# Sums for the norms: fp32 products of the squares in place of reduced products of their two parts

## The chip, the cores and the metric

The kernel runs on one core of one Trainium2 chip. The metric is the device time of one execution in microseconds.

## What is computed

Two transformer blocks run one after the other on 512 tokens of 1024 features, all in fp32. The change concerns the norms of both blocks. There are norms over all features, over the 128 features of a head and over its 64 features:

```python
def rms_norm_2(x, g):
    xf = x.astype(jnp.float32)
    y = xf * lax.rsqrt(jnp.mean(xf * xf, axis=-1, keepdims=True) + EPS)
    return (y * g.astype(jnp.float32)).astype(x.dtype)

# block 1: differential attention, two softmax maps a head, their difference normed
yb = rms_norm(yb, diff_subln_g[l], SUBLN_EPS) * (1.0 - lam_init)
x = x + rms_norm(merged @ w_out[l], norm_mix_post_g[l])
h = rms_norm(x, norm_ffn_pre_g[l])
f = (jax.nn.silu(h @ w_gate[l]) * (h @ w_up[l])) @ w_down[l]
x = x + rms_norm(f, norm_ffn_post_g[l])
# block 2: gated linear attention beside dilated attention
o = rms_norm_2(o, norm_g).reshape(B, S, H * GLA_DV)
qa = rms_norm_2(aq.reshape(B, S, ATTN_HEADS, ATTN_HEAD_DIM), q_norm_g[l])
ka = rms_norm_2(ak.reshape(B, S, ATTN_HEADS, ATTN_HEAD_DIM), k_norm_g[l])
```

## The kernel before, in words

Activations lie feature-major: a tile has 128 features on the partitions and 512 tokens in its columns. Dense products take 128x128 weight tiles, streamed in chunks of eight (L237), and are exact to fp32 by parts: each operand is a high part in the reduced format fp32r and a low part, the remainder (ScalarE copies, VectorE subtracts; L251 and L125 for the weights), and a product is three reduced products (`mm3`): high by high, high by low, low by high.

A norm needs sums over the features, so over the partitions. `square` makes the squares on ScalarE; where several feature tiles are summed, GpSimd or VectorE adds their squares first (`gather`, L320). `parts` splits the squares: a copy on ScalarE to `sqh` (L308), a subtraction on VectorE to `sql` (L125). `colsum` then takes 128 tokens at a time as weights and two columns of ones as the moving operand, once with the high and once with the low part; the sums are in the PSUM bank `pc`, a token to a partition. `headsum` does the same with `hsel`, whose two columns each select half of the partitions: for norms over 64 features, and for the diagonal of the linear attention. A group of sums for 512 tokens is eight products. From the bank follow `rstd` (VectorE L334, GpSimd L336), transposes that spread the factors again (`bcast`; for 64-feature norms the copy at L1267 and transposes), and the scaling.

The program is emitted by a planner. Tasks (one head's attention, a norm, a linear attention's levels) are generators; each `yield t` says that its next TensorE work is ready t us later, on a clock `pt` that the planner advances by an assumed cost of each TensorE instruction (`pin`). Ready tasks go first, tiles of dense products fill the rest, and the order found so is fixed on TensorE. The other engines take their instructions in the order in which they are emitted. Each engine runs in order and waits by semaphores.

The stages, in us of the profile: the start and block 1's attention up to about 340, its branch products, the bridge to the feed-forward around 400 to 440, the feed-forward to 720, the bridge to block 2 to 830, block 2's mixer (linear attention, dilated attention) to 1100, a third bridge to 1150, and the last feed-forward. A bridge (`bridge`) computes the last tiles of a product in two halves of 256 tokens, so that one half's norm lies beside the other's products; its norm is `chain`. In the bridge to block 2 three sums are taken at once (`a0`, `a1`, `a2`). In the mixer, `near` makes decayed queries and keys for one level of the linear attention, `gla` multiplies them into masked scores (twelve products of 128 columns a level), `qk_norm` norms the queries and keys of the dilated attention. `decay` holds the only full fp32 products, 16 rows of weights by 512 columns, for the gates.

Of the kernel before, what the change touches and what calls it, by code (L numbers as in the profile page):

```python
# [19 lines left out]
TB = S // 128  # L20
# [22 lines left out]
# cost of a transpose on the tensor engine, for the order in which its work is issued  # L43
# [3 lines left out]
class Done:  # L47
    """Marks a piece of work as issued; `at` is when its result should be there."""
# [10 lines left out]
class Item:  # L59
    """A dense tile product: runs whenever no task has tensor work that is ready."""  # L60
# [5 lines left out]
class Emitter:  # L66
# [25 lines left out]
    def phase(self, order=range(NSLOT)):  # L92
        """A part of the program with its own use of the working tiles."""
        self.slot, self.turn, self.free = {}, {}, list(order)
        self.pfree, self.pslot, self.res["prob"] = [0, 1, 2], {}, 3

    def W(self, tag, dt=F32, b=1, shape=(128, 512)):
        """A working tile; `b` of a tag take turns."""
        n = self.turn[tag] = self.turn.get(tag, -1) + 1
        key = (tag, n % b)  # L100
        if key not in self.slot:
            self.slot[key] = self.free.pop(0)
        return self.t(self.work, list(shape), dt, f"w{self.slot[key]}")

    def prob(self):
        """A tile for the probabilities of a head; free again after drop."""
# [27 lines left out]
    def mm(self, out, lhsT, rhs, start, stop):  # L134
        n = int(np.prod(rhs.shape[1:]))
        us = max(0.106, 0.216 * n / 512) if rhs.dtype == F32R else max(0.5, 1.14 * n / 512)
# [5 lines left out]
    def mm3(self, out, l, r, first=True, last=True):  # L142
        """out (+)= l^T r from exact parts, (hi, lo) each."""
# [65 lines left out]
    def pump(self, stop=None):  # L209
        """Issue until `stop()` (default: no tasks and no dense work are left)."""  # L210
# [29 lines left out]
    def _split(self, h):  # L240
        """Exact parts of half a chunk."""
# [30 lines left out]
    def mtile(self, ps, w, m, rhs, evac):  # L272
        """Generator: ps = W[:, m]^T rhs, then evac(ps); yields after each k."""
# [8 lines left out]
    def kouter(self, cols, rhs, tags=("mm", "mm", "s", "s")):  # L282
        """Several tiles at once, k outermost: starts as soon as rhs[0] is there."""
# [12 lines left out]
    def colsum(self, ps, sq, first=True, last=True, c=0, tbs=range(TB)):  # L296
        """ps[:, 8 c + 2 tb] += per-token sums over the partitions of sq = (hi, lo), whose columns
        begin with the first of the token tiles tbs; the odd columns get the same."""
        for tb in tbs:
            for i in range(2):  # L300
                o = (tb - tbs[0]) * 128
                self.mm(ps[:, 8 * c + 2 * tb:8 * c + 2 * tb + 2], sq[i][:, o:o + 128], self.ones2,
                        first and tb == tbs[0] and i == 0, last and tb == tbs[-1] and i == 1)

    def parts(self, full, dst=None):
        """(hi, lo) of a tile, for its sums."""
        hi, lo = dst or (self.t(self.sm, [128, 512], F32R, t, 1)[:, :full.shape[1]] for t in ("sqh", "sql"))
        self.nc.scalar.copy(hi, full)  # L308
        self.sub(lo, full, hi)
        return hi, lo  # L310

    def squares(self, x):
        """(hi, lo) of x^2, for its sums."""
        return self.parts(self.square(x))

    def gather(self, acc, sq):
        """acc += sq, beside the products; the first piece is the accumulator itself."""
# [5 lines left out]
    def after(self, ins, first):  # L323
        """Issue `ins` behind `first` on the engine that both run on."""
        self.tc.add_manual_dep(ins.ins, first.ins.name, NOSYNC, reason="order")

    def sums(self, ps, n=1, tbs=range(TB)):
        """The per-token sums that colsum left in the first n groups of columns."""
# [10 lines left out]
    def bcast(self, r):  # L339
        """[128 tokens, n] -> [128, 128 n], the same value on all partitions."""  # L340
# [34 lines left out]
    def qk_pair(self, q32, k32):  # L375
        """Stacked exact parts of two heads (rows 0-63 and 64-127) for the score products."""
# [17 lines left out]
    def v_parts(self, ps, rb=None, dst=None):  # L394
        """Task: token-major exact parts of a feature-major value tile in PSUM."""
# [19 lines left out]
    def scores(self, h, qk, bias, out):  # L415
        """Task part: unnormalised probabilities [128, 1280] and 1/sum of one head."""
# [40 lines left out]
    def att_v(self, p, v, cols, y):  # L457
        """Task part: y[d, q] = sum_s v[s, d] p[q, s] for one head."""
# [25 lines left out]
    def block1_mix(self):  # L484
# [77 lines left out]
        def diff(j, box):  # L562
# [29 lines left out]
            sq = self.squares(yr)  # L592
            yield 2.5
# [13 lines left out]
        # start: the first pair with k outermost, while x arrives; the norm follows  # L607
# [5 lines left out]
        acc = self.parts(acc)  # L613
# [17 lines left out]
        # lambda, the same on every partition  # L631
# [73 lines left out]
    def bridge(self, w, rhs, g, slots, evac, chain, cols, h, tags=("mm", "s", "s", "y"), made=()):  # L705
        """The eight tiles of rhs @ W, the last g of them for the first and then for the other half of
        the tokens, and with h the first four tiles of the next stage, likewise: what the norm of one
        half waits for lies beside products of the other half. The weights of tiles that are used
        twice stay in `slots`. evac(m, c, ps) takes a tile (its columns c); chain(t, ps, done) is the
        task that takes the last tile of a half and makes that half of h; `made` are banks with the  # L710
        first tiles."""
# [65 lines left out]
    def block1_rest(self, mg):  # L777
# [23 lines left out]
        def chain(t, c, ps, done):  # L801
# [4 lines left out]
            sq = self.parts(sq)  # L806
            yield 3.5 if t else 2.0
# [27 lines left out]
        self.colsum(pc, self.parts(acc2))  # L835
# [40 lines left out]
        # modulation of block 2 on the vector engine, beside the products  # L876
# [49 lines left out]
        def chain(t, c, ps, done):  # L926
# [11 lines left out]
            d = [self.t(self.sm, [128, 512], F32R, t, b) for t, b in (("sqh", 1), ("sql", 1), ("sq", 2))]  # L938
            d = [(d[0][:, :256], d[1][:, :256]), (d[0][:, 256:], d[1][:, 256:]), (d[2][:, :256], d[2][:, 256:])]
            d = [self.parts(v, p) for v, p in zip((a0, a1, a2), d)]  # L940
            yield 4.0
            pc = self.bank("pc")
            for i in range(3):
                self.colsum(pc, d[i], i == 0, i == 2, i, tbs)
            # x + f g r has the squares' sum |x|^2 + 2 r x.fg + r^2 |fg|^2
# [39 lines left out]
    def ada(self, k, x, rb, i, dst, t=None):  # L985
        """Exact parts of x * rb * gm + shift, per feature."""
# [8 lines left out]
    def headsum(self, ps, sq):  # L995
        """ps[:, 2 tb + e] = per-token sums over the two halves of the partitions."""
        for tb in range(TB):
            for i in range(2):
                self.mm(ps[:, 2 * tb:2 * tb + 2], sq[i][:, tb * 128:(tb + 1) * 128], self.hsel, i == 0, i == 1)
# [596 lines left out]
```

## Time and profile before

| | |
|---|---|
| median of 3 timed runs | 1505.06 us (1501.72 to 1508.11) |
| profiled execution, span | 1504.9 us |
| TensorE busy | 1451.4 us (96%) |
| VectorE busy | 934.4 us (62%) |
| ScalarE busy | 708.5 us (47%) |
| GpSimd busy | 307.7 us (20%) |
| mean granted clock of TensorE | 0.985 |

The profiled execution has no other time of its own than its span. Busy time is the sum of instruction times by engine; matmuls overlap in the pipeline, so the distance between the starts of two of them says what one costs in a row. A wait names the instruction whose end released the waiting one. The granted clock is 1.00 at 2.4 GHz and 0.50 at 1.2 GHz. In rows, PE is TensorE, PEld its weight loads, DVE VectorE, ACT ScalarE, POOL GpSimd; an operand list reads out<-in, with the moving operand ahead of the weights.

### The profile page before, as it was taken

Reading aid. Unit: us, or ns where it says so; the run is one execution under the profiler, and the core shown is the slowest. Engines: PE = TensorE matmul, PEld = TensorE weight load, DVE = VectorE, ACT = ScalarE, POOL = GpSimd, SP = SyncE. Lnnn points to the kernel's source line nnn. Section 1 sums busy time; section 2 is a strip of 40 time slices with the busy share of each in tenths; the row PEclk is TensorE's granted clock in tenths of the full one; section 3 lists DMA queues with packets and bytes.
Section 4 is the critical chain, followed back from the end, with each engine's and each line's share of the span. In section 5 each row is a group of like instructions: output and inputs, shape, how many; then the busy total and the mean of one; then the engine's idle time right before and its main releaser. Section 6 shows DMA issues by size and latency. Waiting matters only on the chain.

```text
span 1504.9 us, 19407 instructions
## 1 busy us (share of the span) xinstructions
PE 1451.4 (96%) x7054; PEld 1180.6 (78%) x7054; DVE 934.4 (62%) x1753; ACT 708.5 (47%) x1370; POOL 307.7 (20%) x285
## 2 busy tenths in 40 slices
PE   7999999999999999999998879899999999999998
PEld 6777777788988777888797667777779888888887
DVE  6655665656468888542548697766656766665322
ACT  5656655553643222332336546576546444444221
POOL 5322122101261111110314343412210111111000
PEclk9999999999999999999999987999999999999999
DMA  4221222224307887333234101121222233333331
GB/s 168 71 71 56 70 71 70 84 84 154 127 29 231 270 271 248 112 99 97 85 107 146 42 29 41 30 85 50 77 86 69 86 97 98 98 99 98 119 112 64
DMA packets 44592, 154.38 MB, mean 103 GB/s; under 512 B 5088, under 2 KB 5616, under 8 KB 44496
## 3 DMA queue, kind: packets, MB, share of 16 engines
q1 hardware_dynamic: 42944, 148.41, 31.6%
q0 software_dynamic: 1408, 4.59, 1.0%
q8 instruction: 55, 0.90, 0.2%
q14 instruction: 41, 0.34, 0.1%
q10 hardware_dynamic: 144, 0.14, 0.0%
HBM read 148.93 MB, written 4.19 MB: 102 GB/s over the span
## 4 chain that ended last, share of the span: by engine, by line
PE 74%; DVE 10%; issue 5%; DMA 4%; ACT 3%; POOL 3%; SPq 0%; DVEq 0%; POOLq 0%; ACTq 0%
PE mm L137 59%; PE s L137 8%; PE y L137 3%; DMA p<-w_ada 3%; DVE w L125 2%; PE pt L140 2%; POOL w L320 1%; DMA wraw<-w 1%; DVE wlo L125 1%; PE pc L137 1%; DVE w L891 1%; PE pt L137 1%; DVE w L1113 1%; ACT whi L251 1%; POOL rr L336 0%
## 5 line engine op out<-in xcount | busy, mean ns | idle before, releaser
L137 PE MATMUL mm<-hh,whi 128*128 128x512 f32 x1096 | 449.4, 410 | 12.6 <-ACT hh L370 7.0
L125 DVE TENSOR_TENSOR wlo<-wraw,whi 128x512 fp32r<-128x512 f32 x410 | 297.5, 729 | 252.4 <-ACT whi L251 248.7
L251 ACT CAST whi<-wraw 128x512 fp32r<-128x512 f32 x410 | 250.5, 620 | 399.4 <-PE mm L137 284.7
L137 PE MATMUL mm<-hl,whi 128*128 128x512 f32 x1096 | 431.3, 394 | 0.0
L137 PE MATMUL mm<-hh,wlo 128*128 128x512 f32 x1096 | 431.3, 394 | 0.0
L137 PE MATMUL mm<-w,whi 128*128 128x512 f32 (+1 forms) x984 | 281.5, 371 | 2.2 <-ACT w L1318 0.9
L137 PEld LDWEIGHTS mm<-hh,whi 128*128 128x128 f32 x1096 | 207.7, 189 | 69.5 <-issue 20.5
L137 PEld LDWEIGHTS mm<-hh,wlo 128*128 128x128 f32 x1096 | 207.7, 190 | 45.1
L137 PEld LDWEIGHTS mm<-hl,whi 128*128 128x128 f32 x1096 | 208.2, 190 | 36.2 <-DVE hl L371 0.6
L137 PEld LDWEIGHTS mm<-w,whi 128*128 128x128 f32 x984 | 177.4, 188 | 34.7 <-ACT w L1318 1.3
L137 PE MATMUL mm<-w,wlo 128*128 128x512 f32 (+1 forms) x492 | 181.5, 369 | 1.6 <-DVE wlo L125 1.6
L137 PEld LDWEIGHTS mm<-w,wlo 128*128 128x128 f32 x492 | 92.7, 188 | 17.5 <-DVE wlo L125 2.0
L137 PE MATMUL s<-w,w 128*128 128x128 f32 (+3 forms) x364 | 94.4, 352 | 8.1 <-DVE w L1196 5.2
L125 POOL TENSOR_TENSOR w<-w,w 64x512 fp32r<-64x512 f32 x48 | 66.6, 1387 | 142.4 <-ACT w L384 92.5
L137 PEld LDWEIGHTS s<-w,w 128*128 128x128 f32 x364 | 62.1, 206 | 39.8 <-issue 31.9
L891 DVE SCALAR_TENSOR_TENSOR w<-p,p 128x1024 bf16<-128x1024 f32 x48 | 63.7, 1327 | 20.5 <-DMA p<-w_ada 20.2
L125 DVE TENSOR_TENSOR w<-pt,w 128x512 fp32r<-128x512 f32 (+3 forms) x106 | 52.9, 505 | 34.5 <-ACT w L468 29.0
L1453 POOL TENSOR_TENSOR w<-w,w 128x512 f32<-128x512 f32 x22 | 29.0, 1319 | 205.6 <-ACT w L1452 205.5
L428 DVE CUSTOM_DVE_ANT_0 p<-s,w 128x128 f32<-128x128 f32 (+1 forms) x96 | 46.8, 488 | 35.4 <-PE s L137 34.7
L848 POOL TENSOR_TENSOR w<-w,w 128x512 f32<-128x512 f32 x22 | 28.6, 1304 | 193.6 <-ACT w L847 193.6
L320 POOL TENSOR_TENSOR w<-w,w 128x256 f32<-128x256 f32 (+1 forms) x43 | 48.8, 1138 | 91.6 <-ACT w L355 56.7
L125 DVE TENSOR_TENSOR w<-w,w 128x512 fp32r<-128x512 f32 (+3 forms) x107 | 59.5, 567 | 11.3 <-ACT w L859 4.8
(273 smaller groups left out, 1910.2 us busy)
## 6 DMA issues: line engine op xcount, KB each, us to landing
wraw<-w SPq DMA_DIRECT2D x220, 512.0 KB, 3.6
p<-w_ada SPq DMA_DIRECT2D x48, 512.0 KB, 4.4
x<-xT SPq DMA_DIRECT2D x8, 256.0 KB, 6.2
x<-xT POOLq DMA_DIRECT2D x8, 256.0 KB, 2.9
xd<-x SPq DMA_DIRECT2D x8, 256.0 KB, 2.5
x<-xd POOLq DMA_DIRECT2D x8, 256.0 KB, 2.9
outT<-x SPq DMA_DIRECT2D x7, 256.0 KB, 2.1
p<-c SPq DMA_DIRECT2D x1, 512.0 KB, 3.6
```

Of the source, the lines that this page charges most:

```text
L125: (eng or self.nc.vector).tensor_tensor(out=out, in0=full, in1=hi, op=ALU.subtract)
L137: self.pin(self.nc.tensor.matmul(out, lhsT=lhsT, rhs=rhs, start=start, stop=stop), us)
L140: self.pin(self.nc.tensor.transpose(out, in_, self.ident), USTR)
L251: self.nc.scalar.copy(hi, raw)
L320: self.nc.gpsimd.tensor_tensor(out=acc, in0=acc, in1=sq, op=ALU.add)
L428: nc.vector.tensor_tensor_reduce(out=p[:, OFF[i]:OFF[i] + w], in0=ps[:, :w], in1=bias[:, 384 - 128 * i:512], op0=ALU.add, op1=ALU.max, sca ...
L848: nc.gpsimd.tensor_tensor(out=g, in0=g, in1=sg, op=ALU.mult)
L891: nc.vector.scalar_tensor_tensor(out=junk, in0=wa, scalar=1.0, in1=cond, op0=ALU.mult, op1=ALU.mult, accum_out=self.mod[:, ni:ni + 1])
L1113: nc.vector.tensor_tensor_scan(c[:, o:o + n], self.one256[:, :n], la[p][:, o:o + n], 0.0, op0=ALU.mult, op1=ALU.add)
L1453: nc.gpsimd.tensor_tensor(out=u, in0=u, in1=sg, op=ALU.mult)
```

## The change

The squares go into the sums as they are. `colsum` and `headsum` take one fp32 tile and make one full fp32 product for each 128 tokens, each starting and ending its own accumulation; `parts` and `squares` are gone, and with them the copies and subtractions. The columns of ones and of `hsel` are fp32. The planner's delays ahead of the sums are 1.3 us shorter (1.5 in the bridge to block 2), and its assumed cost of an fp32 product is lower. The diff also removes comments; it is cut to the core here, and one of four alike stands for the head norms.

```diff
     def mm(self, out, lhsT, rhs, start, stop):
         n = int(np.prod(rhs.shape[1:]))
-        us = max(0.106, 0.216 * n / 512) if rhs.dtype == F32R else max(0.5, 1.14 * n / 512)
+        us = max(0.106, 0.216 * n / 512) if rhs.dtype == F32R else max(0.22, 0.86 * n / 512)
...
-    def colsum(self, ps, sq, first=True, last=True, c=0, tbs=range(TB)):
+    def colsum(self, ps, sq, c=0, tbs=range(TB)):
         for tb in tbs:
-            for i in range(2):
-                o = (tb - tbs[0]) * 128
-                self.mm(ps[:, 8 * c + 2 * tb:8 * c + 2 * tb + 2], sq[i][:, o:o + 128], self.ones2,
-                        first and tb == tbs[0] and i == 0, last and tb == tbs[-1] and i == 1)
-
-    def parts(self, full, dst=None):
-        hi, lo = dst or (self.t(self.sm, [128, 512], F32R, t, 1)[:, :full.shape[1]] for t in ("sqh", "sql"))
-        self.nc.scalar.copy(hi, full)
-        self.sub(lo, full, hi)
-        return hi, lo
-
-    def squares(self, x):
-        return self.parts(self.square(x))
+            o = (tb - tbs[0]) * 128
+            self.mm(ps[:, 8 * c + 2 * tb:8 * c + 2 * tb + 2], sq[:, o:o + 128], self.ones, True, True)
...
             yield "sq"
-            sq = self.squares(yr)
-            yield 2.5
+            sq = self.square(yr)
+            yield 1.2
...
             nc.vector.tensor_tensor(out=sq, in0=sq, in1=acc[:, c], op=ALU.add)
-            sq = self.parts(sq)
-            yield 3.5 if t else 2.0
+            yield 2.2 if t else 0.7
...
-        self.colsum(pc, self.parts(acc2))
+        self.colsum(pc, acc2)
...
-            d = [self.parts(v, p) for v, p in zip((a0, a1, a2), d)]
-            yield 4.0
+            yield 2.5
             pc = self.bank("pc")
-            for i in range(3):
-                self.colsum(pc, d[i], i == 0, i == 2, i, tbs)
+            for i, v in enumerate((a0, a1, a2)):
+                self.colsum(pc, v, i, tbs)
...
         for tb in range(TB):
-            for i in range(2):
-                self.mm(ps[:, 2 * tb:2 * tb + 2], sq[i][:, tb * 128:(tb + 1) * 128], self.hsel, i == 0, i == 1)
+            self.mm(ps[:, 2 * tb:2 * tb + 2], sq[:, tb * 128:(tb + 1) * 128], self.hsel, True, True)
...
             nc.gpsimd.tensor_tensor(out=t, in0=q, in1=k, op=ALU.mult)
-            t = self.parts(t)
-            yield 5.5
+            yield 4.2
...
         def qk_norm(w, f, box, done):
             yield "sq"
-            sq = self.squares(f)
-            yield 4.0
+            sq = self.square(f)
+            yield 2.7
```

The order of TensorE moves wherever a delay is shorter. Two places follow. The first is TensorE in the mixer, at the first head norm of the dilated attention; s is the bank of the linear attention's masked scores, of which the last three of twelve stand here, pc the bank of the sums, whose pair of a high and a low part comes four times. Before:

```order
L137 MATMUL s_7720<-w_1612_7496,w_1610_7494 128x128
L137 MATMUL s_7720<-w_1613_7497,w_1610_7494 128x128
L137 MATMUL s_7720<-w_1612_7496,w_1611_7495 128x128
L137 MATMUL pc_7747<-hsel_95,sqh_7692 128x2
L137 MATMUL pc_7747<-hsel_95,sql_7693 128x2
```

In the changed kernel, at the same norm, with the last dense product (mm) ahead of the sums and the first three of the twelve scores behind them:

```order
L137 MATMUL mm_7579<-hh_1539_7040,whi_7477 128x512
L137 MATMUL mm_7579<-hl_1540_7041,whi_7477 128x512
L137 MATMUL mm_7579<-hh_1539_7040,wlo_7478 128x512
L137 MATMUL pc_7599<-hsel_89,sq_7577 128x2 x4
L137 MATMUL s_7610<-w_1588_7402,w_1586_7400 128x128
L137 MATMUL s_7610<-w_1589_7403,w_1586_7400 128x128
L137 MATMUL s_7610<-w_1588_7402,w_1587_7401 128x128
```

The group of sums is one row of four and stands ahead of the twelve score products, no longer behind them.

The second is VectorE in the bridge to block 2, at the second half's sums; the p and rbc tiles are the halves of the feed-forward's output, hl low parts of the next stage's input, pt the spread factors. Before:

```order
L125 TENSOR_TENSOR hl_1550_7062<-p_1389_6102,hh_1549_7061 128x256
L937 TENSOR_TENSOR w_1395_6108<-w_1395_6108,w_1552_7071 128x256
L125 TENSOR_TENSOR sql_7076<-w_1393_6106,sqh_7075 128x256
L125 TENSOR_TENSOR sql_7076<-w_1394_6107,sqh_7075 128x256
L125 TENSOR_TENSOR sq_7077<-w_1395_6108,sq_7077 128x256
L962 TENSOR_TENSOR p_1390_6103<-p_1390_6103,pt_7023 128x256
L990 TENSOR_TENSOR p_1389_6102<-x_846_3455,pt_7040 128x256
L125 TENSOR_TENSOR w_1561_7112<-wraw_6932,w_1560_7111 128x512
L962 TENSOR_TENSOR rbc_6104<-rbc_6104,pt_7023 128x256
L990 TENSOR_TENSOR p_1390_6103<-x_847_3456,pt_7040 128x256
L125 TENSOR_TENSOR hl_1559_7103<-p_1389_6102,hh_1558_7102 128x256
```

In the changed kernel, from the low part ahead of the accumulators' last additions:

```order
L125 TENSOR_TENSOR hl_1529_6983<-p_1371_6038,hh_1528_6982 128x256
L919 TENSOR_TENSOR w_1531_6992<-dm_6041,x_838_3415 128x256
L920 SCALAR_TENSOR_TENSOR w_1376_6043<-sq_6988,gsq_98,w_1376_6043 128x256
L922 TENSOR_TENSOR w_1377_6044<-w_1377_6044,w_1531_6992 128x256
L125 TENSOR_TENSOR w_1537_7024<-wraw_6859,w_1536_7023 128x512
L125 TENSOR_TENSOR hl_1535_7015<-p_1371_6038,hh_1534_7014 128x256
L944 TENSOR_TENSOR rbc_6040<-rbc_6040,pt_6929 128x256
L972 TENSOR_TENSOR p_1372_6039<-x_835_3412,pt_6948 128x256
L929 COPY pv_7053<-pc_7046 128x6
L944 TENSOR_TENSOR dm_6041<-dm_6041,pt_6929 128x256
L321 TENSOR_SCALAR rv_7055<-pv_7053 128x2
```

The three subtractions are gone, the sums' evacuation (L929, L321) follows among the first half's work, and L919 to L922 add into the accumulators that TensorE then reads.

## Rows read from the trace of the kernel before

**Rows 1.** Busy time of the engines, from the page (share of the span, instructions)

```profile
PE 1451.4 (96%) x7054; PEld 1180.6 (78%) x7054; DVE 934.4 (62%) x1753; ACT 708.5 (47%) x1370; POOL 307.7 (20%) x285
```

**Rows 2.** Stretches: length, busy us of each engine, granted clock, DMA

```profile
35.00:340.00 305.00, 303.85 (x1414) 232.84 (x1413) 188.63 (x422) 185.54 (x376) 64.25 (x46) 1.00 0.24 71
...
830.00:1100.00 270.00, 247.90 (x1225) 192.32 (x1223) 190.72 (x435) 159.48 (x347) 86.09 (x85) 0.92 0.17 49
...
850.00:892.00 42.00, 30.64 (x169) 25.41 (x168) 35.33 (x74) 21.95 (x45) 21.98 (x23) 0.96 0.17 51
892.00:919.00 27.00, 25.15 (x72) 18.35 (x73) 21.02 (x54) 13.89 (x35) 8.64 (x11) 0.50 0.07 19
...
790.00:815.00 25.00, 18.10 (x134) 16.66 (x133) 23.27 (x61) 15.93 (x34) 8.68 (x13) 0.97 0.36 118
```

**Rows 3.** TensorE waits, whole span, then 830 to 1100: total, times, longest

```profile
PE pc L137 <- DVE sql L125: 5.5, 7, 2.8
...
PE pc L137 <- ACT sqh L308: 1.7, 2, 1.4
...
PE pt L140 <- DVE sqh L1267: 4.2, 2, 2.2
PE pc L137 <- DVE sql L125: 3.3, 2, 2.8
...
PE pc L137 <- ACT sqh L308: 1.4, 1, 1.4
```

**Rows 4.** Forms of the sums products: busy us, mean ns, idle before

```profile
L137 PE MATMUL pc<-ones,sql 128*128 128x2 f32 x56 | 13.1, 253 | 2.7 <-DVE sql L125 2.7
...
L137 PE MATMUL pc<-hsel,sql 128*128 128x2 f32 x40 | 9.2, 251 | 3.0 <-DVE sql L125 2.8
...
L137 PE MATMUL pc<-ones,sq 128*128 128x2 f32 x8 | 1.2, 250 | 0.0
```

**Rows 5.** Timeline around the first group: start, us, engine, operation

```profile
27.47 0.19 PEld L137 LDWEIGHTS pc<-ones,sqh 128*128 128x128 f32 x1
27.70 0.17 PE L137 MATMUL pc<-ones,sqh 128*128 128x2 f32 x1
27.70 0.19 PEld L137 LDWEIGHTS pc<-ones,sql 128*128 128x128 f32 x1
...
28.37 0.19 PEld L137 LDWEIGHTS pc<-ones,sql 128*128 128x128 f32 x1
...
28.48 0.19 PEld L137 LDWEIGHTS s<-hh,whi 128*128 128x128 f32 x1
```

**Rows 6.** Fp32 products of the gates beside reduced ones; weight loads around partial rows

```profile
L137 PE MATMUL s<-w,wlo 128*128 128x512 f32 x76 | 29.6, 389 | 0.0
...
L137 PE MATMUL s<-w,w 16*128 16x512 f32 x4 | 2.0, 613 | 0.0
...
833.15 0.29 PEld L137 LDWEIGHTS s<-w,w 16*128 16x128 f32 x2 [0.35 <-issue]
...
59.94 0.18 PEld L137 LDWEIGHTS s<-w,w 64*128 64x128 f32 x1 [0.31 <-issue]
```

**Rows 7.** Weight loads of four transposes, timeline

```profile
30.44 0.59 PEld L140 LDWEIGHTS pt<-ident,rr 128*128 128x128 f32 x4
```

**Rows 8.** The copies and subtractions: ns min/median/max, first and last start

```profile
L308 ACT CAST sqh<-sq x20: 389/617/622, 212.3 to 1143.0; 128x512 fp32r<-128x512 f32 x16, 128x256 fp32r<-128x256 f32 x4
L125 DVE TENSOR_TENSOR sql<-sq,sqh x20: 418/684/1549, 213.3 to 1143.7; 128x512 fp32r<-128x512 f32 x16, 128x256 fp32r<-128x256 f32 x4
L308 ACT CAST sqh<-w x8: 392/516/621, 25.4 to 902.2; 128x512 fp32r<-128x512 f32 x4, 128x256 fp32r<-128x256 f32 x4
L125 DVE TENSOR_TENSOR sql<-w,sqh x8: 409/555/693, 26.1 to 902.8; 128x512 fp32r<-128x512 f32 x4, 128x256 fp32r<-128x256 f32 x4
```

**Rows 9.** Pieces of the chain of waits: start us, us, what

```profile
797.06 0.67 DVE sql L125 x2
797.73 0.34 DVE sq L125
...
852.99 2.44 DVE w L1182 x8
...
855.76 0.60 DVE sql L125
...
870.47 1.03 DVE sql L125
...
963.89 0.60 DVE sql L125
```

**Rows 10.** Table loads of ScalarE ahead of the exponentials

```profile
L438 ACT ACT_TABLE_LOAD x11 | 14.1, 1283 | 0.2
```

More of the change, by code (lines that the diff above doesn't have):

```diff
@@ L612, in block1_mix @@
             acc = self.gather(acc, self.square(x[k], T(f"gb{k}")))
-        acc = self.parts(acc)
         for k, _ in enumerate(self.mtile(self.bank("s"), "w_in", 24, h, e_gate(0))):
@@ L937, in chain @@
             nc.vector.tensor_tensor(out=a2, in0=a2, in1=tt, op=ALU.add)
-            d = [self.t(self.sm, [128, 512], F32R, t, b) for t, b in (("sqh", 1), ("sql", 1), ("sq", 2))]
-            d = [(d[0][:, :256], d[1][:, :256]), (d[0][:, 256:], d[1][:, 256:]), (d[2][:, :256], d[2][:, 256:])]
-            d = [self.parts(v, p) for v, p in zip((a0, a1, a2), d)]
-            yield 4.0
+            yield 2.5
             pc = self.bank("pc")
-            for i in range(3):
-                self.colsum(pc, d[i], i == 0, i == 2, i, tbs)
+            for i, v in enumerate((a0, a1, a2)):
+                self.colsum(pc, v, i, tbs)
             pv = self.t(self.sm, [128, 3, 2], F32, "pv")
@@ L1242, in gla_norm @@
             yield "sq"
-            sq = self.squares(o)
-            yield 2.5
+            sq = self.square(o)
+            yield 1.2
             pg = self.bank("pc")
@@ L1420, in chain @@
             nc.vector.tensor_tensor(out=sq, in0=sq, in1=acc[:, c], op=ALU.add)
-            sq = self.parts(sq)
-            yield 5.0 if t else 2.4
+            yield 3.7 if t else 1.1
             pc = self.bank("pc")
@@ L1501, in run @@
             nc.gpsimd.memset(self.one256, 1.0)
-            self.ones2 = C([128, 2], "ones2", F32R)
-            nc.vector.tensor_copy(self.ones2, self.ones)
-            hsel = C([128, 2], "hself")
-            nc.vector.memset(hsel, 0.0)
-            nc.vector.memset(hsel[0:64, 0:1], 1.0)
-            nc.vector.memset(hsel[64:128, 1:2], 1.0)
-            self.hsel = C([128, 2], "hsel", F32R)
-            nc.vector.tensor_copy(self.hsel, hsel)
+            self.hsel = C([128, 2], "hsel")
+            nc.vector.memset(self.hsel, 0.0)
+            nc.vector.memset(self.hsel[0:64, 0:1], 1.0)
+            nc.vector.memset(self.hsel[64:128, 1:2], 1.0)
             self.mhalf = C([128, 16], "mhalf")
```

## The prediction

> **What bounds the kernel now.** I read the busy line of the page first. TensorE is busy for 1451.4 us of a span of 1504.9 us, VectorE for 934.4, ScalarE for 708.5 [rows 1]: the time is TensorE's work plus some 53 us in which it stands. Then the stages, to see where it stands [rows 2]. In block 1's attention (35 to 340) it is busy 303.85 of 305 us, so nothing taken from another engine can show there. In block 2's mixer (830 to 1100) it is busy 247.9 of 270: 22 us of standing, the largest piece. There VectorE sets the pace: busy 35.3 of the 42 us from 850 to 892, while TensorE stands 11.4. The second place is the bridge from the feed-forward of block 1 to block 2 (790 to 815), VectorE busy 23.3 of 25, TensorE 18.1. Behind the first of these TensorE runs for 27 us at a granted clock of 0.50, its lower level of 1.2 GHz.
>
> Last the waits: what the change takes away ends 7.2 us of TensorE's standing, 5.5 for the low parts on VectorE and 1.7 for the high parts on ScalarE; 4.7 of these 7.2 lie in the mixer [rows 3].
>
> **The products.** Before there are 200 sums products of two columns: 56 and 40 with low parts, as many with high parts, and 8 whose low or high part has the name sq [rows 4]. Their pace is that of their weight loads: of a group of eight the first load begins at 27.47 and the load behind the group at 28.48, and from 27.70 to 28.48 the other seven take 0.78, so 0.112 us each [rows 5]. 200 by 0.112 is 22.4 us. Afterwards there are 100 products in full fp32. The only such products in the trace are the two of the gates' projection: four records, so two for each product, each of 613 ns against 389 for a reduced one of as many columns [rows 6]. The 224 ns between are one more passage of the 512 columns; with two columns that is next to nothing, and what is left is two weight loads a product. The second load of the pair starts 0.11 us behind the first (two loads of 0.18 in 0.29). So 100 by 2 by 0.112 is 22.4 again: no change, my value. Bounds: a transpose, also fp32 data, has one load a tile, at 0.148 us (four in 0.59) [rows 7]; 100 of these would be 14.8, a gain of 7.6. From above, if the second load of each pair waits until the first product is out, 250 ns [rows 4], it is 100 by (0.250 - 0.112), 13.8 us more.
>
> A smaller cost at the edges: the first fp32 load shows 0.35 us of standing with no releaser [rows 6], where reduced products of 128 rows show none [rows 5]. A reduced product with 64 rows of weights shows 0.31 of the same kind [rows 6], and the gates' projection has 16 rows. So I put it down to the rows, not to fp32, and take 0; the upper bound is 0.31 for each of the 26 groups of sums, 8.1 us.
>
> The page "FP8 and Floating Point Precision" of the Trainium skill (section TensorE Precision Notes) says that true fp32 takes four passes. The longer records agree with four passes. If each pass brought a weight load of its own, there would be 400 loads; the rows show two a product.
>
> **The parts.** 30 pairs of a ScalarE copy and a VectorE subtraction go: 20 of 512 columns at 617 and 684 ns, 10 of 256 at some 400 [rows 8], some 16 us of ScalarE and 18 of VectorE. Only what the end waits for counts. I take it from the chain of waits [rows 9]. In the mixer three subtractions lie on it, 0.60, 1.03 and 0.60: 2.2 us. In the bridge at 790 to 815 the three of the second half lie on it, 0.67 and 0.34: 1.0 us. Outside the mixer the waits for the parts, 7.2 less 4.7, are 2.5 us [rows 3]: one in block 1's last head norms, the rest at the first and third bridge and at the sum of the residual. Sum 5.7. I do not add the 4.7 in the mixer: there VectorE is late anyway, so TensorE meets the next wait for it, such as the spread of a head norm's factors, for which it stands 4.2 us [rows 3]. The lower bound of this gain is 0 (every wait taken up by the next), the upper one 2.5 + 4.7 + 1.0 and as much again in the bridge's first half, 9.2.
>
> **The order.** The planner's delays for the sums are 1.3 us shorter, the length of a copy and a subtraction, so in the written order the sums come forward by as much. For the first head norm of the mixer they now stand ahead of the twelve masked-score products and no longer behind them. There TensorE waited 2.8 us for the subtraction [rows 3], which was queued behind eight diagonal scalings on VectorE [rows 9]; now it can wait only for the square on ScalarE. What is late next there is VectorE's parts for the twelve products. In the second bridge the sums leave VectorE's queue, and the updates behind them move up by three instructions. ScalarE gets two more table loads of 1.28 us [rows 10], in block 1, where it is busy 185.5 of 305 us [rows 2]; that cover hides them, and 2.6 us is the price without it. Three tiles (the accumulators, the squares, the diagonal's product) are now read by TensorE and come free one group of sums later, about 1 us; the next writer stands behind those sums in each case, so 0. No DMA is added, removed or moved past another on its queue.
>
> **The sum.** 1504.9 - 5.7 + 0 = 1499.2 us. The profiled span lies 0.2 us under the median of the three timed runs, 1505.06, so nothing outside the span has to be added.
>
> **The rivals.**
>
> *The half-clock stretch goes (faster).* TensorE stands 11.4 of the 42 us ahead of 892, then gets half its clock for 27 us, in which it is busy 25.15 [rows 2]. If the shorter waits ahead of it keep the clock up, that stretch needs 12.6 us of TensorE, but VectorE is busy 21.0 in it: 6.0 to 12.6 gained, say 9. Time 1490. For it: two of the three subtractions on the chain lie just ahead of it, and the 2.8 us wait. Against: VectorE's other work keeps TensorE waiting there too.
>
> *The second load of a pair is not hidden (slower).* Each fp32 product loads its weights twice into the same rows of the array. If the second load must wait for the first product, 13.8 us are added, all on the engine that bounds the kernel: 1504.9 - 5.7 + 13.8 = 1513. It decides against the change from a distance of 0.17 us between the loads of a pair (0.112 + 5.7/100). For it: these records are few in the trace, and have 16 rows of weights where the sums have 128. Against: the distance of 0.11 [rows 6].
>
> In the Trainium skill, "TensorE: Matmul & The Clock Gate" (section The mechanism) holds that a weight load overlaps a matmul in flight only when their row groups differ. By that rule this rival would hold. The trace does not bear it out: with equal rows the load of the first sums product starts at 27.47, with the product ahead of it in flight, and the product itself at 27.70 [rows 5].
>
> *Four loads a product (slower).* If 128 rows bring four loads, 22.4 us more: 1522.
>
> *The waits only move (no change).* The sums wait for the square, or the next product for VectorE, by as much as was saved: 1505. For it: in the mixer each wait is followed by another for VectorE.
>
> **How the numbers follow.** The forecast of 1499.2 has a chance of 0.36, its own range 1494 to 1504; the clock's rival 0.27 (1490); the hidden load 0.17 (1513); four loads 0.04 (1522); moved waits 0.16 (1505). About half a per cent, 7.5 us, is what a measurement of this kernel can tell from no change: below 1497.5 is faster, above 1512.6 slower. Faster: a third of the forecast's 0.36, nearly all of the clock's 0.27, 0.39 together. Slower: half of the hidden load's 0.17, all of the 0.04, 0.02 from moved waits, 0.15. Same: 0.46. The range 1487 to 1515 leaves out the deeper end of the clock's rival, below, and the four loads with the upper end of the hidden load's, above.
>
> **What would show it.** Right: two records a sums product, loads 0.11 us apart; no high or low part among the waits; VectorE's busy time lower by some 18 us and ScalarE's by some 13; TensorE's standing in the mixer down from 22 us by two or three; the half clock still there. Wrong: loads 0.17 us or more apart within a pair, or 400 of them; standing ahead of and behind each group of sums; the half-clock stretch at 892 gone, or a new one elsewhere; or a wait for the square as long as that for the subtraction was.

## The result and the profile after

The changed kernel takes 1518.25 us, median of 7 runs (1511.73 to 1520.39), beside 1506.98 for the kernel before on the same chip (1501.72 to 1512.94, 7 runs): ratio 1.0077, 95% interval 1.0054 to 1.0101, slower by 0.8%. The forecast was 1499.2 us, its range 1487 to 1515. The profiled run took 1520.39 us.

The page's busy line, which answers to [rows 1]:

```profile
PE 1460.9 (96%) x7054; PEld 1188.0 (78%) x7054; DVE 912.9 (60%) x1721; ACT 696.7 (46%) x1342; POOL 309.4 (20%) x285
```

VectorE gave up 21.5 us and ScalarE 11.8, near the 18 and 13 that the 30 pairs of copy and subtraction were to bring. TensorE has as many records as before and is busy 9.5 us longer. The stretches of [rows 2]:

```profile
35.00:340.00 305.00, 304.10 (x1415) 233.07 (x1414) 184.04 (x418) 185.90 (x375) 64.68 (x46) 1.00 0.24 71
830.00:1100.00 270.00, 248.57 (x1183) 194.03 (x1181) 175.74 (x410) 148.24 (x321) 85.44 (x85) 0.88 0.17 49
850.00:892.00 42.00, 32.63 (x160) 27.04 (x160) 32.77 (x71) 20.91 (x44) 24.37 (x25) 0.83 0.13 38
892.00:919.00 27.00, 25.91 (x74) 19.00 (x75) 17.99 (x49) 11.38 (x27) 6.47 (x8) 0.50 0.13 39
790.00:815.00 25.00, 21.57 (x162) 20.66 (x160) 20.62 (x58) 14.75 (x32) 9.47 (x13) 0.93 0.37 109
```

The mixer (830 to 1100) stands as long as before, 21.4 us against 22.1, yet shows 42 records of products fewer, at a granted clock of 0.88 in place of 0.92. From 850 to 892 the clock is 0.83 where it was 0.96. Block 1's attention is unchanged.

The sums products, by form (duration in ns: least, median, most; first and last start), against [rows 4]; and the first group's weight loads, against [rows 5]:

```profile
L137 PE MATMUL pc<-ones,sq x80: 168/251/354, 213.3 to 1155.9; 128*128 128x2 f32 x80
L137 PE MATMUL pc<-hsel,sq x64: 169/251/272, 851.9 to 1068.1; 128*128 128x2 f32 x64
L137 PE MATMUL pc<-ones,w x40: 165/251/251, 27.6 to 800.9; 128*128 128x2 f32 x40
L137 PE MATMUL pc<-hsel,w x16: 165/251/251, 844.5 to 922.7; 128*128 128x2 f32 x16
```

```profile
27.35 1.08 PEld L137 LDWEIGHTS pc<-ones,w 128*128 128x128 f32 x8
28.36 0.19 PEld L137 LDWEIGHTS s<-hh,whi 128*128 128x128 f32 x1
```

80, 64, 40 and 16 are 200 records, two for each fp32 product, and the group holds TensorE for 1.01 us from its first load to the load behind it, as before.

TensorE's waits from 830 to 1010 (total, times, longest), against [rows 3]:

```profile
PE pt L140 <- ACT w L386: 5.9, 2, 3.6
PE s L137 <- DVE w L1176: 4.3, 2, 2.4
PE pt L140 <- DVE w L125: 3.6, 1, 3.6
PE pc L137 <- ACT sq L342: 3.2, 2, 3.0
PE y L137 <- ACT w L1203: 2.4, 1, 2.4
```

No part is among them, but the 2.8 us for the first head norm's low part has become 3.0 for its square. Of the others, that for the masked copies (L1176) stood at 5.2 us before, as L1196, and the rest are new or longer; none of them but `sq` is an operand of the sums. This is the first group of head sums, and ScalarE at that time:

```profile
848.35 0.39 PE L137 MATMUL mm<-hl,whi 128*128 128x512 f32 x1
848.58 0.39 PE L137 MATMUL mm<-hh,wlo 128*128 128x512 f32 x1
851.95 1.05 PE L137 MATMUL pc<-hsel,sq 128*128 128x2 f32 x8 [2.98 <-ACT sq L342]
852.86 1.31 PE L137 MATMUL s<-w,w 128*128 128x128 f32 x10
```

```profile
850.10 0.59 ACT L1266 COPY w<-mm 128x512 f32<-128x512 f32 x1
850.75 0.63 ACT L1115 ACTIVATE w<-w 128x512 f32<-128x512 f32 x1
851.28 0.61 ACT L342 ACTIVATE sq<-w 128x512 f32<-128x512 f32 x1
```

The sums were issued for a square that ScalarE had still to make, behind the copy of the tile (its input) and an exponential of the linear attention. The masked-score products (`s`) stand behind the sums. With the old delays (e_old_delays below) the same sums stand behind those products, and the square directly behind the copy on ScalarE; they wait for nothing:

```profile
848.82 1.44 PE L137 MATMUL s<-w,w 128*128 128x128 f32 x11 [0.45 <-DVE w L125]
850.10 1.00 PE L137 MATMUL pc<-hsel,sq 128*128 128x2 f32 x8
```

```profile
848.04 0.63 ACT L342 ACTIVATE sq<-w 128x512 f32<-128x512 f32 x1
```

### The profile page after: what moved, and what is told of

Its sections match the earlier page's. It is cut to its first block, busy times and chain, and to the rows that moved or that the text cites. A ratio compares the mean times of both kernels' runs of the same rounds, so it can differ in the third digit from the quotient of the medians.

```text
span 1517.8 us, 19346 instructions
## 1 busy us (share of the span) xinstructions
PE 1460.9 (96%) x7054; PEld 1188.0 (78%) x7054; DVE 912.9 (60%) x1721; ACT 696.7 (46%) x1342; POOL 309.4 (20%) x285
## 4 chain that ended last, share of the span: by engine, by line
PE 76%; DVE 8%; DMA 6%; issue 4%; ACT 3%; POOL 2%; DVEq 0%; POOLq 0%; ACTq 0%; SPq 0%
PE mm L137 60%; PE s L137 8%; DMA p<-w_ada 4%; PE y L137 3%; PE pt L140 2%; DMA wraw<-w 2%; DVE w L125 2%; PE pc L137 1%; DVE wlo L125 1%; PE pt L137 1%; DVE w L876 1%; DVE w L1094 1%; POOL w L307 1%; POOL rr L323 0%; DVE w L1162 0%
## 5 line engine op out<-in xcount | busy, mean ns | idle before, releaser
L137 PE MATMUL s<-w,w 128*128 128x128 f32 (+3 forms) x364 | 97.7, 363 | 4.3 <-DVE w L1176 4.3
L415 DVE CUSTOM_DVE_ANT_0 p<-s,w 128x128 f32<-128x128 f32 (+1 forms) x96 | 46.8, 488 | 45.2 <-PE s L137 44.8
```

Of the source, the lines that this page charges most:

```text
L137: self.pin(self.nc.tensor.matmul(out, lhsT=lhsT, rhs=rhs, start=start, stop=stop), us)
L415: nc.vector.tensor_tensor_reduce(out=p[:, OFF[i]:OFF[i] + w], in0=ps[:, :w], in1=bias[:, 384 - 128 * i:512], op0=ALU.add, op1=ALU.max, sca ...
```

## The experiments

All ratios are to the kernel before, run beside each, with 95% intervals. "Delay" is the number after which the planner takes an operand of the sums to be there. The old delays, with `-` for the changed kernel's:

```diff
-            yield 1.2      # block 1's head norms
+            yield 2.5
-            yield 2.2 if t else 0.7   # first bridge
+            yield 3.5 if t else 2.0
-            yield 2.5      # second bridge
+            yield 4.0
-            yield 4.2      # mixer: diagonal of the linear attention
+            yield 5.5
-            yield 1.2      # mixer: norms of its heads (gla_norm)
+            yield 2.5
-            yield 2.7      # mixer: norms of the attention heads (qk_norm)
+            yield 4.0
-            yield 3.7 if t else 1.1   # third bridge
+            yield 5.0 if t else 2.4
```

**Data or order: e_old_delays, e_parts_new_delays, e_mixer_old_delays.** The first has the fp32 sums with all old delays, and a cost of 0.212 us for a sums product in the planner, so that TensorE's order is that of before:

```diff
-        us = ... max(0.22, 0.86 * n / 512)
+        us = ... (0.212 if n == 2 else max(0.5, 1.14 * n / 512))
```

The second is the kernel before, parts and all, with the new delays and costs. The third is the changed kernel with the three mixer delays of before. In the traces the 7054 TensorE records of e_old_delays come in the order of the kernel before, and those of e_parts_new_delays in the order of the changed kernel, record by record, where a pair of a high and a low product answers to the two records of an fp32 product.

> Fp32 sums of the squares, but with the planner's delays and assumed costs of before, so that TensorE's order is that of before, each pair of a high and a low product being one fp32 product. Theory 1 (the new order of the mixer costs the time, by standing at other places and by the half clock that follows): 1495 to 1503 us, faster than before by 4 to 11, the half-clock total between 830 and 1010 us at or under the 41 us of before. Theory 2 (the fp32 sums themselves cost it, as products or by their wait for the square on ScalarE): 1514 to 1521, as the changed kernel.

> The kernel before, sums from two parts, but with the shorter delays and the assumed costs of the changed kernel, so that TensorE's order is the changed one. Theory 1 (order): 1514 to 1526 us, as slow as the changed kernel or slower, since the parts come 1.3 us later than the order allows for. Theory 2 (the fp32 sums themselves): 1503 to 1510, as before.

> The changed kernel with the delays of before in block 2's mixer alone (diagonal, gated norm, query and key norms); the bridges keep the shorter ones. Theory 1 (the mixer's order): 1495 to 1504 us, the bridge to block 2 as early as in the changed kernel (some 6 us gained there) and the mixer no longer than before. Theory 2 (the fp32 sums themselves): 1514 to 1521.

Measured: 0.9971 (0.9955 to 0.9986), 1.0257 (1.022 to 1.0294), 1.0006 (0.999 to 1.0022). So the fp32 sums gain 0.3% in the old order, and the new order costs: 1.0077/0.9971 is 1.1% with fp32 sums, 2.6% with parts, whose copy and subtraction the shorter delays leave no time for (1542.5 us, far above the 1514 to 1526 expected). Two thirds of the 1.1% come back with the mixer's delays. One expectation of e_old_delays failed: its half clock from 830 to 1010 us was to be at or under 41 us and is 47.8.

**Which delay: e_qk_old, e_glanorm_old, e_diag_old, e_norms_old.** The changed kernel with one of the mixer's delays of before; the last with the two of the norms.

> The changed kernel with one delay of before: that of the eight norms of attention heads in the mixer (4.0 in place of 2.7). Of the three mixer delays, all three restored together gave 1.0006 against the changed kernel's 1.0077. Theory A (one place: in the changed kernel the mixer's loss opens after 970 us, where the head norms and the last linear-attention heads lie, so these norms' sums stand too early): 1.000 to 1.003, half-clock stretches back near 45 us. Theory B (each delay costs its share): 1.004 to 1.006. Theory C (any shift of the order moves the time, not these sums in particular): could be anything, also above 1.008.

> The changed kernel with one delay of before: that of the norms of the linear attention's heads (2.5 in place of 1.2). Theory A (the eight norms of the attention heads cost it): 1.006 to 1.008, nothing back. Theory B (shares): 1.004 to 1.006; these norms come at 945 to 1045 us, so what comes back must come back behind 945. Theory C: anything.

> The changed kernel with one delay of before: that of the linear attention's diagonal sums (5.5 in place of 4.2). Up to the linear attention's level at 969 us the changed kernel is level with the kernel with all delays of before but for 2 to 3 us. Theory A (the norms of the attention heads cost it): 1.005 to 1.008. Theory B: 1.004 to 1.006. Theory C: anything.

> The changed kernel with two delays of before, those of the attention heads' norms and of the linear attention's heads' norms; the diagonal's stays short. If the delays add up (1.0077 less 0.0026 and 0.0039): 1.001. With the diagonal's too it was 1.0006, so 1.000 to 1.003. If they do not add up: above 1.004, and then the diagonal's delay costs only together with the others.

Measured: 1.0051 (1.0031 to 1.0071), 1.0038 (1.0018 to 1.0059), 1.009 (1.0057 to 1.0123), 1.0047 (1.0027 to 1.0066). Theory A, one place, falls by e_glanorm_old, which was to bring nothing back. Against the changed kernel's 1.0077 that gain is just clear of the noise; that of e_qk_old is not, and both together bring no more than one. The delays don't add up.

**How much: e_half, e_longer.** The kernel with the old delays, its mixer delays 0.65 us shorter (half the change), and 1.3 us longer:

```diff
-            yield 5.5
+            yield 4.85     # e_longer: 6.8
-            yield 2.5
+            yield 1.85     # e_longer: 3.8
-            yield 4.0
+            yield 3.35     # e_longer: 5.3
```

> The fp32 sums with all delays of before, but the three mixer delays shortened by half of what the change takes (0.65 us each). Theory 'shorter is dearer' (each step to shorter delays adds standing and half clock in the mixer): between 0.9971 and about 1.004 (0.9971 plus half of the 0.0071 that the three delays cost is 1.0007). Theory 'any shift deals the time anew': 0.997 plus or minus 0.01, with no relation to the size. In either, the time over the kernel with the delays of before should be its extra TensorE standing plus half of its extra busy time at half clock, within 3 us.

> The fp32 sums with all delays of before outside the mixer and the three mixer delays 1.3 longer than before (6.8, 3.8, 5.3). The kernel with the delays of before measured 0.9971. If sums that stand ahead of their operand are what costs time in the mixer and some still do at the old delays (TensorE stood 18 us there), longer ones gain again: 0.993 to 0.996. If the old delays were at their best, or the sums then hold back the norms that follow: 0.998 to 1.004. If any shift of the order is as good as another, 0.997 plus or minus 0.01.

Measured: 1.0051 (1.0031 to 1.0071) and 0.9995 (0.9977 to 1.0014). Half the step costs as much as the whole (e_mixer_new below, 1.005). Its median lies above what "shorter is dearer" allowed, though its interval reaches into that, and within "any shift deals anew". The opposite step gains nothing: 0.9995 lies above 0.9971 at the edge of the noise, as was expected if the old delays were at their best. The pair of 0.9971 and 1.0051 also shows at one place how an order costs time. Up to the linear attention's level at 943 us both kernels keep within 2 us of each other at these levels. Then, in e_half, TensorE's and VectorE's rows:

```profile
965.53 0.65 PE L137 MATMUL s<-w,w 128*128 128x128 f32 x2
966.12 0.50 PE L137 MATMUL mm<-hh,whi 128*128 128x512 f32 x1
966.45 0.39 PE L137 MATMUL mm<-hl,whi 128*128 128x512 f32 x1
966.68 0.40 PE L137 MATMUL mm<-hh,wlo 128*128 128x512 f32 x1
971.08 1.06 PE L137 MATMUL s<-w,w 128*128 128x256 f32 x2 [4.01 <-DVE mx L415]
```

```profile
969.04 0.69 DVE L125 TENSOR_TENSOR w<-w,w 128x512 fp32r<-128x512 f32 x1 [1.26 <-ACT w L1123]
969.65 1.28 DVE L1176 COPY_PREDICATED w<-w,s 128x256 f32<-128x256 uint8 x2
970.74 0.20 DVE L321 TENSOR_SCALAR rv<-pc 128x4 f32<-128x4 f32 x1
970.79 0.28 DVE L415 CUSTOM_DVE_ANT_0 p<-s,w 128x128 f32<-128x128 f32 x1
```

and TensorE's in e_old_delays:

```profile
966.71 0.40 PE L137 MATMUL mm<-hh,wlo 128*128 128x512 f32 x1
967.77 1.53 PE L137 MATMUL s<-w,w 128*128 128x128 f32 x12 [0.66 <-DVE rv L321]
969.13 0.85 PE L137 MATMUL y<-w,w 128*64 128x512 f32 x3
969.83 0.38 PE L140 MATMUL pt<-ident,p 128*128 128x128 f32 x2
970.04 0.60 PE L140 MATMUL pt<-ident,rr 128*128 128x128 f32 x4
970.40 0.68 PE L137 MATMUL s<-w,w 128*128 128x256 f32 x2
```

The two score products of an attention head (128x256) stand behind a level's twelve products in the better kernel and start at 970.40 without a wait. In e_half they stand ahead of the twelve. There they wait for VectorE's reduction of the score tile before them (L415, 970.79), and in VectorE's queue that one stands behind the linear attention's masked copies (L1176) and a subtraction that waits for ScalarE. TensorE stands 4.01 us, the twelve products behind it. VectorE's chain was late by then: the same subtraction comes 5.0 us earlier in e_old_delays,

```profile
964.01 0.69 DVE L125 TENSOR_TENSOR w<-w,w 128x512 fp32r<-128x512 f32 x1
```

so the place shows how an order turns a late chain into standing, not what made the chain late. The next stretch, first of e_old_delays and then of e_half:

```profile
970.00:1010.00 40.00, 40.00 (x200) 30.83 (x199) 25.34 (x60) 26.33 (x58) 5.05 (x6) 1.00 0.31 92
```

```profile
970.00:1010.00 40.00, 38.92 (x169) 29.46 (x170) 24.85 (x59) 24.50 (x54) 3.75 (x5) 0.87 0.24 73
```

169 records against 200, most of it by the clock, which is at half for 10.2 us behind the 4.01 us of standing.

**The sums or what hangs on them: e_mixer_new, e_sums_early, e_follow_early.** The kernel with the old delays, changed in three ways: the mixer's three new delays; these, and the step behind each kind of sums (the diagonal's first level, the broadcast of the factor, the turning of the spread factors) 1.3 us later; the old delays, and these steps 1.3 us earlier.

```diff
     # e_sums_early (new delays)    e_follow_early (old delays)
-                yield 3.5
+                yield 4.8 if li == 0 else 3.5     # 2.2
-            yield 2.5
+            yield 3.8                             # 1.2
-            yield 4.5
+            yield 5.8                             # 3.2
```

> The fp32 sums with all delays of before except the three in the mixer, which are the changed kernel's. It is the reference for the two other runs. The changed kernel, with all new delays, measured 1.0077, the one with all old ones 0.9971. If the mixer's delays cost it nearly all: 1.004 to 1.009. If they cost only together with those outside: 0.997 to 1.003.

> As the kernel with only the mixer's new delays, but the step behind each of the three kinds of sums waits 1.3 us longer, so the sums come early and what hangs on them at its old time. Theory 'followers' (the steps moved past the linear attention's products do the harm): 0.996 to 1.001. Theory 'sums' (the sums do it, ahead of their square): 1.004 to 1.009, as the reference. Theory 'any change of the order costs': 1.002 to 1.006.

> The mirror image: all delays of the sums as before, but the step behind each of the three kinds of sums in the mixer waits 1.3 us less, so the sums stand where they did and what hangs on them comes early. Theory 'followers': 1.004 to 1.010. Theory 'sums': 0.996 to 1.000. Theory 'any change of the order costs': 1.002 to 1.006.

Measured: 1.005 (1.0031 to 1.0069), 1.0023 (1.0007 to 1.004), 1.0075 (1.0049 to 1.01). With the followers at their old time a third of the 0.0079 is back; with the followers alone brought forward the loss is 0.0104, which can't be told from the 0.0079 of both. "Sums" alone falls by the last run, "followers" alone by the one before it, where TensorE still waits 3.0 us for `sq`. Each does harm, and together they cost less than the two losses added up. Which does more isn't shown: e_follow_early puts the followers closer to the sums than the changed kernel does, and TensorE waits there for what is made from the sums, 5.6 us for `rr` (L323) and 3.6 for `sqh` (L1247), which are not among the changed kernel's waits above.

**Outside the mixer: e_old_blk1, e_old_br1, e_old_b2, e_old_br3.** The kernel with the old delays, one place outside the mixer with the changed kernel's.

> The fp32 sums with all delays of before except that of block 1's head norms (1.2 in place of 2.5). The kernel with the old delays in the mixer alone measured 1.0006 against 0.9971 with all, so some 5 us lie outside the mixer. Theory 'block 1': 1.000 to 1.001, with the feed-forward stage beginning 2 us later. Theory 'bridges': 0.996 to 0.998, no change.

> The fp32 sums with all delays of before except that of the first bridge (0.7 and 2.2 in place of 2.0 and 3.5). If the 5 us outside the mixer lie here: 0.999 to 1.001, lost at 390 to 460 us and in the feed-forward behind it. If not: 0.996 to 0.998.

> The fp32 sums with all delays of before except that of the second bridge (2.5 in place of 4.0), where the changed kernel needed some 2 us less from the feed-forward to the mixer than the kernel with the delays of before. If that gain holds to the end: 0.995 to 0.997, the best version. If the mixer takes it up: 0.997 to 1.000. If the second bridge's delay is what costs outside the mixer: 1.000 or more.

> The fp32 sums with all delays of before except that of the third bridge (1.1 and 3.7 in place of 2.4 and 5.0). The changed kernel lost 2 to 3 us there, with half clock at 1103. If these are the delay's: 0.998 to 1.000. If they only follow from what the mixer left undone: 0.996 to 0.998.

Measured: 0.9964 (0.9946 to 0.9982), 0.9959 (0.9938 to 0.9981), 0.9967 (0.9947 to 0.9986), 0.9979 (0.9956 to 1.0003): none differs from 0.9971. What all four cost together (e_mixer_old_delays at 1.0006) is no sum of these; it stays open. The lower assumed costs, which e_mixer_old_delays has as well, are not the reason: its order of TensorE differs from that of e_old_delays at the places of the four runs and at no other.

**The clock: e_fill.** The changed kernel with 58 products that nobody reads (24, 15, 9 and 10 at four places), ahead of instructions for which TensorE stood 2.98, 3.63, 2.29 and 2.37 us.

```diff
+    def fillup(self, out, count):
+        n = out.shape[1]
+        for _ in range(count):
+            self.pin(self.nc.tensor.matmul(out, lhsT=self.idle[:, :128], rhs=self.idle[:, :n],
+                                           start=True, stop=True), 0.0)
```

> The changed kernel with 58 products that nobody reads, put where TensorE stood in its trace: 24 of 256 columns ahead of the first query norm's sums (2.98 us stood), 15 and 9 of 512 ahead of the transposes of the second and third value tile of the mixer (3.63 and 2.29), 10 ahead of the second linear-attention head's first product (2.37). They fill waiting and keep the order. If the half clock that follows the standing is the price: half-clock time between 840 and 940 us falls from 48 us to under 20, and the time to 1500 to 1511. If the waits themselves are the price and not the clock: 1516 to 1522, with the half clock gone or not.

Measured: 1.0125 (1.0102 to 1.0149), 1522.2 us, at the upper edge of what was expected if the waits are the price. The other products keep their order. From 830 to 1010, the changed kernel and then e_fill:

```profile
830.00:1010.00 180.00, 160.36 (x733) 125.64 (x732) 126.46 (x288) 98.70 (x208) 62.85 (x67) 0.82 0.14 41
```

```profile
830.00:1010.00 180.00, 159.91 (x792) 128.01 (x792) 127.49 (x290) 97.74 (x208) 62.24 (x67) 0.89 0.14 42
```

The clock rose from 0.82 to 0.89 (half clock from 840 to 940 us: 23.9 us, not under 20 as expected, and 41.5 in the changed kernel) and the standing remained 20 us: the four waits all but went (0.6 us are left), and others came (3.4, 3.4, 3.3, 3.1 us elsewhere). The gates' first product, where the mixer begins, and a level of the linear attention, in the changed kernel and then in e_fill:

```profile
825.09 0.40 PE L137 MATMUL pc<-hh,w 128*16 128x512 f32 x1
972.23 1.54 PE L137 MATMUL s<-w,w 128*128 128x128 f32 x12
```

```profile
821.26 0.40 PE L138 MATMUL pc<-hh,w 128*16 128x512 f32 x1
972.29 1.54 PE L138 MATMUL s<-w,w 128*128 128x128 f32 x12
```

The stretch took 147.1 us, and 151.0 with the filling and the higher clock. So the clock that these products kept up gave nothing back; whether one kept up without the products' own time would, this run doesn't show.

**An account of all runs.** For each profile I added up TensorE's standing between its first and last record, and half of its busy time in stretches at half clock (1.2 of 2.4 GHz). What half clock is for the pace of dense products, the changed kernel shows: they start 0.43 us apart here, and 0.23 apart at 848 above.

```profile
968.25 0.63 PE L137 MATMUL mm<-hh,wlo 128*128 128x512 f32 x1
968.68 0.63 PE L137 MATMUL mm<-hh,whi 128*128 128x512 f32 x1
```

What is left of the last record's end is its work at full clock, with the 7 us ahead of its first record:

| kernel | last end | standing | half of busy at half clock | rest |
|---|---|---|---|---|
| before | 1500.5 | 42.1 | 21.2 | 1437.2 |
| e_old_delays | 1494.4 | 38.6 | 19.8 | 1436.0 |
| e_half | 1508.6 | 40.6 | 35.0 | 1433.0 |
| changed | 1513.4 | 45.6 | 34.4 | 1433.4 |
| e_follow_early | 1513.7 | 46.4 | 33.0 | 1434.2 |
| e_parts_new_delays | 1544.1 | 53.0 | 56.8 | 1434.3 |
| e_fill | 1512.7 | 45.1 | 22.0 | 1445.6 |

The rest is 1433 to 1437.5 in all kernels but e_fill, which carries its 58 products (some 11 us). So the changed kernel's 12.9 us over before are 3.5 more standing, 13.2 more half clock and 3.8 less rest. For e_half over e_old_delays standing and half clock make 17.2 us, and 14.2 were measured, just within the 3 us that its expectation allowed. It is an account, not a cause: e_fill has 12.4 us less half clock than the changed kernel, no less standing, and ends 0.7 us sooner.

Each row is one execution; those of the changed kernel and of e_parts_new_delays are their slowest, that of e_fill its fastest. Over all executions, the span times one less the granted clock is at most what half clock took: 34.2 us in the mean for the changed kernel and 21.6 for e_old_delays, and the remainder of the span is 1481.2 and 1475.4. For the kernel before, beside e_old_delays, they are 20.4 and 1481.3. So the parts' removal shows as 5.9 us of the remainder in the old order; in the new order the remainder is back where it was, and the half clock comes on top.

## Why the prediction was wrong

*The products, 0 us: right.* 200 records at the old pace. The rivals with a load that waits (13.8 us) or four loads fall: eight loads and the start of a ninth in 1.01 us, though one product takes 0.25. The rule of the Trainium skill, "TensorE: Matmul & The Clock Gate" (section The mechanism), that a load overlaps a product in flight only where the row groups differ, isn't borne out for fp32 with 128 rows either. The same section also lets a load into the background weight buffer go ahead of products in flight, which these rows don't speak against.

*The parts, -5.7: right in size.* With the order held, the ratio 0.9971 is 4.4 us less (2.1 to 6.8). Where in the kernel it is gained isn't shown: the gates' first product comes at 822.4 us in e_old_delays and at 826.1 before, but at 823.1 to 827.3 in the profiles of five other kernels with fp32 sums and the same order up to there (e_half, e_follow_early, e_longer, e_mixer_new, e_sums_early).

*The order, 0: this step failed.* It said that "the sums come forward by as much", looked at one place, and named what is late next there without a price. It cost 1.1% (1.0077 over 0.9971), some 16 us. Two things were missing. At the place that it did look at, the wait for the square was given no price; it was 2.98 us, as long as the 2.8 for the subtraction, since ScalarE makes the square behind the copy of the tile and an exponential. That was among the signs named for a wrong forecast. And the steps behind the sums (the factor, its spread, the scores) moved forward with them, past products of the linear attention. By e_sums_early they are about a third of the mixer's loss. Of the 19.4 us of waits listed above for the changed kernel (830 to 1010), all but 3.2 are for something other than a sum's operand; which move made each of them was not traced.

*The clock's rival, 0.27 for 1490: the right stretch, the wrong sign.* The half-clock stretch behind 892 did not go: 888 to 919 in the changed kernel. Others came, at 874 (6.8 us), and 963 (6.8) and 977 (13.7) in place of one of 6.8 at 970. The changed kernel's half clock is 71.7 us in all, 44.4 before.

*The waits only move, 0.16 for 1505: half right.* Standing in the mixer went from 22.1 to 21.4 us, not down by two or three, and in the whole kernel from 42.1 to 45.6. The rival's price had no term for the clock behind the new places.

The better version is e_old_delays, 0.3% faster than the kernel before; the variants with one outside delay shortened can't be told from it.

## What to carry to other kernels

When a change makes an operand ready earlier and a planner's delay is shortened with it, measure the two apart: hold the old order first. A delay moves every step behind it too, so read off the order what each of them now stands ahead of, and which engine's queue its operand is in. Here the sum of the waits that go (5.7 us) came out with the order held, and the order's move cost nearly three times as much.

## What the runs showed that was not expected

Equal standing can bring very different clocks. From 820 to 1010 us e_old_delays stands 16.8 us and e_half 17.1, yet TensorE's busy time at half clock is 39.6 and 59.6 us there. In e_old_delays 11.9 of the 16.8 lie in two waits:

```profile
862.64 1.11 PE L140 MATMUL pt<-ident,sqh 128*128 128x128 f32 x4 [6.72 <-DVE sqh L1247]
863.40 0.78 PE L137 MATMUL mm<-hh,whi 128*128 128x512 f32 x1
```

The half clock of 10.2 us there begins at 857.3, so more than half of it falls on the standing itself and costs nothing. In e_half six waits of 1.0 to 5.1 us are spread over 120 us, and 10.2 us of half clock fall behind the one at 971 on work. Whether spreading is the cause was not tried by itself.
